# A hybrid encoder layer on one core: residual rows and norm weights loaded with the output projection, values' stores held one round, two weight places added within the value group

## The chip, the cores and the metric

The kernel runs on one core of a Trainium2 chip. The metric is the time of one execution on the device, in microseconds, as the median of several runs. The engines are named as in the profile: PE is TensorE (matmuls and transposes), DVE is VectorE, ACT is ScalarE, POOL is GpSimd, SP is SyncE, which here only issues DMAs. POOL and ACT issue some DMAs too.

## What is computed

One encoder layer, for a prompt of 1024 tokens (A) and a sample of 512 tokens (B) with the same weights, in float32. The reference, cut to its frame:

```python
def encoder_layer(x, pre_w, w_in, conv_w, conv_b, i_bias, f_bias, head_norm_w, w_pm, w_pa, w_out, post_w, rel_table):
    h = rms_norm(x, pre_w)
    cols = jnp.einsum('bsd,dc->bsc', h, w_in)
    m_qk, m_v, m_o, m_z, m_i, m_f, a_qkv, a_z, gate = jnp.split(cols, np.cumsum(IN_SPLITS)[:-1], axis=-1)
    y_m = mlstm_mixer(m_qk, m_v, m_o, m_i, m_f, ...) * jax.nn.silu(m_z)
    y_a = dilated_attention(a_qkv, rel_table) * jax.nn.silu(a_z)
    p_m = jnp.einsum('bsc,cd->bsd', y_m, w_pm)
    p_a = jnp.einsum('bsc,cd->bsd', y_a, w_pa)
    g = jax.nn.sigmoid(gate).reshape(b_, s_, N_BRANCHES, D_MODEL)
    merged = g[:, :, 0] * p_m + g[:, :, 1] * p_a
    out = jnp.einsum('bsd,de->bse', merged, w_out)
    return x + rms_norm(out, post_w)
```

The model is 1024 wide; the combined input projection gives queries, keys and values for a bidirectional mLSTM (4 heads of 256) and for attention in three dilation groups of 8 heads of 64, and the gates. "Values" below are the columns of `m_v` and of the attention's v. The residual rows are the `x` of the last line; the last norm's weights are `post_w`.

## The kernel before

Every large product is made of three matmuls with operands split in a high and a low part (`mm3`, L199 to L203): high times high, high times low, low times high. A weight is therefore loaded as raw float32 (`load_w`), copied to its high part on ACT (L261) and subtracted to its low part on DVE (L265); both are in `split_w`, which keeps the two instructions in `self.splits`. Raw weights have two buffers, `wraw`; split weights rotate through a list of places, `wsplit`, three by default: the front one is taken and put back at the end. `retired` lists places that are dropped when they come to the front.

The program has two halves. First A's input projection runs dense. Then follows a part in which the attention and the mLSTM of one batch form a main thread, and dense work of the other is the *fill*: A's mLSTM, A's attention, B's mLSTM, B's attention, and the end, with `STEPS` = 316, 260, 192, 290 and 86 fill steps planned for each. A fill step is three matmuls of a weight unit. `Fill.stage` spreads a stage's steps over its shares, and `fill(share)` runs the steps that have come due. The fill's order is: B's input projection in units of 8 steps, 40 of them ahead of B's values; the values (192 steps); the rest of B's projection, to step 768 (`SHORT`); then for each block of 512 tokens the two branch projections (`branches`) and the output projection (`final`).

`Fill.load` splits further weights ahead of their use: never more than `ahead` (2; 4 in the last two stages) beyond those taken, and never more than there are places. `base` counts the weights that are no longer needed.

The values (`value_units`) come in six groups of 430 columns. A group has four weights, each for two of the eight contraction blocks, and four token tiles; `slot` walks through tiles and weights so that the next tile begins two slots after the one before it. The four weights of a group stay until its last tile has used them, and so the group needs more places than three. Two more come from the arena tiles `X0` and `X1`, free between A's mLSTM and B's. When a token tile has its eight blocks, `put` in `value_units` copies it from PSUM to `sw` (L779 and L786 on ACT, L780 on DVE) and stores it to `vs` (mLSTM values, high and low part) or `av` (attention values). `sw` is a rotation of four buffers, shared with the other units. A PSUM bank (two for `dense`) is free only after these copies.

Stores in these stages are not issued at once. `Net.put` appends them to `pending` with the round at which they become due, `clock + lag`; `lag` is 2 or 3, in the attention 3. `tick`, at the start of every round of the main thread, issues the queued loads of that round and then the stores that have come due (L217). A store is issued earlier if its buffer's turn in the rotation comes again.

The main thread of the attention (`attend`, `att_round`) has 96 rounds for A and 48 for B. A round computes the logits of one tile (`lg`, L1308), the softmax of the tile before (L1320, L1322 on DVE, L1324 on ACT), transposes the probabilities of the one before that (`pt`, L1331; copied to `pts`, L1334 or L1336), runs its share of fill and makes the output of the oldest (`o`, L1343; L1345). A unit of two heads has 8 rounds in A; the loads for the next unit are queued in a unit's second round and spread over the rest.

The order of work is fixed by hand for PE and SP: they follow the program's order (`manual_schedule`). For ACT, DVE and POOL a planner chooses at compile time, from what is ready in its own simulation. `tc.issue_after(ins)` adds, for each instruction that its block traces on the engine of `ins`, an ordering edge behind `ins`; it orders the issue alone, without a wait, and leaves other engines' instructions as they are.

`side` is the queue on which weights, merge gates, branch rows and residual rows are loaded: SP, but POOL during A's attention and from B's attention on. In the last two stages the pool `out` (`osb`) holds the tiles of the branches and of the output projection, among them `postw`, the norm's weights broadcast to 128 partitions and scaled by ACT (L1907, L1908).

In `final`, a token tile's output has two halves of 512 columns, u = 0 and 1; `close` takes each from PSUM (L1630, L1632, L1637 use `pw`, which is `postw`), and after the second half adds the residual rows `xo` (L1640), which were loaded by L1666 when that half's first contraction blocks were done.

## Time and profile before

| what | value |
|---|---|
| runs | 2278.32, 2275.62, 2276.38 us; median 2276.38 us |
| the profiled execution's own time | 2276.12 us |
| its span, first to last instruction | 2274.3 us |
| granted TensorE clock, mean | 0.998 |
| DMA moved | 418.80 MB, 184 GB/s over the span |
| A's attention, about | 1300 to 1650 us of the span |
| B's values within it | 1351.2 (first L779) to 1580.8 us (last L786) |
| B's attention begins, about | 1845 us |

A row of the timeline gives start, duration, engine and line, what is written from what, and in brackets how long the engine was idle before it and which event ended that. A row of waits gives total, count and longest, in us. A "q" behind an engine's name is its instruction queue. A row for a tile or line gives the least, median and greatest duration in ns, and the first and last start. In the windows view a stretch's length is followed by the busy time of PE, of PE's weight loads, of DVE, ACT and POOL, then the granted clock, the DMA engines' busy share and GB/s.

### The profile page before, as it was taken

How to read it: one execution, taken by the hardware profiler on the slowest of the kernel's cores; microseconds unless marked ns; L12 is line 12 of the kernel's file. 1: busy time of each engine (PE TensorE's matmuls, PEld its weight loads, DVE VectorE, ACT ScalarE, POOL GpSimd, SP SyncE). 2: the span in 40 equal slices, each digit the busy share in tenths (PEclk: the TensorE clock that was granted, in tenths of full speed). 3: DMA queues.
4: the chain of work that ended last, by engine and by line, in shares of the span. 5: the costliest groups of instructions: out<-in, count | busy, mean ns of one | idle time of the engine just before them, and what ended most of it. 6: DMA issues, size and time to landing. Idle time of an engine off the chain costs nothing.

```text
span 2274.3 us, 35427 instructions
## 1 busy us (share of the span) xinstructions
PE 2249.4 (99%) x12226; PEld 1966.9 (86%) x12226; DVE 1505.8 (66%) x2865; ACT 1131.9 (50%) x2368; POOL 723.4 (32%) x1004
## 2 busy tenths in 40 slices
PE   9999999999999999999999999999999999999998
PEld 8999888888888888888888889899888888888887
DVE  6765577677776556467887845444689844655774
ACT  6432244344444334366777655566666644555332
POOL 2000333343333223237666611011065522221230
PEclk9999999999999999999999999999999999999999
DMA  3652555543333223394674589987678787776672
GB/s 122 170 130 78 172 207 194 192 169 119 111 110 108 82 81 136 112 329 130 220 230 143 164 231 252 218 236 226 199 259 282 225 274 232 228 244 195 222 252 84
DMA packets 223213, 418.80 MB, mean 184 GB/s; under 512 B 24857, under 2 KB 129497, under 8 KB 223034
## 3 DMA queue, kind: packets, MB, share of 16 engines
q1 hardware_dynamic: 195064, 316.21, 44.1%
q0 software_dynamic: 24368, 87.74, 12.2%
q10 hardware_dynamic: 3602, 12.59, 1.4%
q8 instruction: 97, 1.59, 0.3%
q14 instruction: 82, 0.67, 0.1%
HBM read 296.45 MB, written 128.39 MB: 187 GB/s over the span
## 4 chain that ended last, share of the span: by engine, by line
PE 87%; DMA 6%; DVE 2%; issue 2%; POOL 2%; ACT 1%; SPq 0%; DVEq 0%; POOLq 0%; ACTq 0%
PE d L203 13%; PE d L201 13%; PE d L202 13%; PE dense L201 10%; PE dense L203 10%; PE dense L202 10%; PE o L1343 4%; PE pt L1331 2%; PE lg L1308 2%; PE num L203 1%; PE num L201 1%; PE num L202 1%; DMA wraw<-w_in 1%; PE kv L201 1%; PE kv L202 1%
## 5 line engine op out<-in xcount | busy, mean ns | idle before, releaser
L201 PE MATMUL dense<-H,wh 128*128 128x512 f32 x664 | 270.4, 407 | 2.7 <-ACT sw L850 2.7
L203 PE MATMUL dense<-H,wl 128*128 128x512 f32 x664 | 260.8, 393 | 0.0
L202 PE MATMUL dense<-H,wh 128*128 128x512 f32 x664 | 260.3, 392 | 0.0
L202 PE MATMUL d<-Hl,phla 128*128 128x512 f32 x608 | 236.5, 389 | 0.0
L203 PE MATMUL d<-Hh,phla 128*128 128x512 f32 x608 | 236.5, 389 | 0.0
L201 PE MATMUL d<-Hh,phla 128*128 128x512 f32 x608 | 236.5, 389 | 0.0
L265 DVE TENSOR_TENSOR wl<-wraw,wh 128x1024 fp32r<-128x1024 f32 (+1 forms) x121 | 148.6, 1228 | 105.8 <-ACT wh L261 103.1
L203 PE MATMUL d<-Hh,phlb 128*128 128x512 f32 x456 | 177.4, 389 | 0.0
L201 PE MATMUL d<-Hh,phlb 128*128 128x512 f32 x456 | 177.4, 389 | 0.0
L202 PE MATMUL d<-Hl,phlb 128*128 128x512 f32 x456 | 177.4, 389 | 0.0
L648 POOL TENSOR_TENSOR psum_w<-pw_raw 128x512 f32<-128x512 f32 x38 | 59.1, 1556 | 368.7 <-DMA pw_raw<-w_in 343.5
L261 ACT ACTIVATE wh<-wraw 128x1024 fp32r<-128x1024 f32 (+1 forms) x124 | 128.5, 1036 | 94.2 <-PE dense L202 25.8
L1324 ACT ACTIVATE ls<-ls,nm 128x256 f32<-128x256 f32 (+1 forms) x288 | 130.1, 453 | 84.9 <-DVE nm L1322 64.0
L1320 DVE CUSTOM_DVE_ANT_0 ls<-lg,bias 128x256 f32<-128x256 f32 (+1 forms) x288 | 93.5, 361 | 118.7 <-PE lg L1308 48.9
L203 PEld LDWEIGHTS dense<-H,wl 128*128 128x128 f32 x664 | 124.7, 188 | 28.2
L201 PE MATMUL d<-vhi,Hh 128*128 128x322 f32 x448 | 140.9, 314 | 0.3
L203 PE MATMUL d<-vhi,Hl 128*128 128x322 f32 x448 | 140.2, 313 | 0.4 <-DVE Hl L370 0.2
L201 PEld LDWEIGHTS dense<-H,wh 128*128 128x128 f32 x664 | 125.0, 188 | 17.3 <-ACT sw L850 2.9
L202 PE MATMUL d<-vlo,Hh 128*128 128x322 f32 x448 | 139.6, 311 | 0.0
L202 PEld LDWEIGHTS dense<-H,wh 128*128 128x128 f32 x664 | 125.4, 189 | 14.3
L201 PEld LDWEIGHTS d<-Hh,phla 128*128 128x128 f32 x608 | 114.1, 188 | 23.7
L203 PEld LDWEIGHTS d<-Hh,phla 128*128 128x128 f32 x608 | 114.1, 188 | 23.7
(564 smaller groups left out, 6169.7 us busy)
## 6 DMA issues: line engine op xcount, KB each, us to landing
pw_raw<-w_in SPq DMA_DIRECT2D x76, 512.0 KB
wraw<-w_in SPq DMA_DIRECT2D x64, 512.0 KB
aqk_a<-pwk SPq DMA_DIRECT2D x48, 512.0 KB
aqk_b<-sw SPq DMA_DIRECT2D x48, 256.0 KB
wraw<-w_pm POOLq DMA_DIRECT2D x24, 512.0 KB, 6.3
wraw<-w_out POOLq DMA_DIRECT2D x24, 512.0 KB, 4.4
wraw<-w_v POOLq DMA_DIRECT2D x23, 430.0 KB, 5.9
erep<-erow SPq DMA_DIRECT2D x16, 512.0 KB
```

Of the source, the lines that this page charges most:

```text
L201: nc.tensor.matmul(out, lh, rh, start=start, stop=False)
L202: nc.tensor.matmul(out, lh, rl, start=False, stop=False)
L203: nc.tensor.matmul(out, ll, rh, start=False, stop=stop)
L261: high = nc.scalar.activation(hi[:, :n], raw[:, :n], AF.Copy)
L265: low = (self.lows or nc.vector).tensor_sub(lo[:, :n], raw[:, :n], hi[:, :n].bitcast(F32))
L648: self.nc.gpsimd.tensor_add(s[:, 0], ws[1][:, 0], ws[1][:, 1])
L1308: nc.tensor.matmul(lg[:, hh, c:c + w], q[hh][:, qs], z[:, k0:k0 + w], start=z is k[hh], stop=z is not k[hh])
L1320: nc.vector.tensor_tensor_reduce(out=ls[:, hh], in0=ts["lg"][hh], in1=bt[:, hh], scale=1.0, scalar=NEG, op0=OP.add, op1=OP.max, accum_out= ...
L1324: nc.scalar.activation(ls[:, hh], ls[:, hh], AF.Exp, bias=nm[:, hh:hh + 1], accum_out=ot[:, 128 + hh:129 + hh])
L1331: nc.tensor.transpose(pp[:, hh * nk + x], ts["ls"][:, hh, x * P:(x + 1) * P], self.ident)
L1343: nc.tensor.matmul(po[:, hh * 64:hh * 64 + 64], pt[:, hh * nk + x], v[:, kt[x], c0 + hh * 64:c0 + hh * 64 + 64], start=x == 0, stop=x == n ...
```

## The change

There are four edits. `put` takes a `lag` of its own, and the three stores of `value_units` pass 1. The places in `X0` and `X1` are taken at slot 1 of the value unit, and are inserted into `wsplit` behind its free places, instead of being appended after A's mLSTM; `retired` is set from a local list. The residual rows' loads stand in `issue_after(self.splits[1].ins)`. The norm's weights are no longer loaded on SP ahead of B's attention, but in the first `final`, on `side`, in the same kind of block; their tile is allocated there, and ACT scales it there.

```diff
-    def put(self, key, out, src, of, queue=None):
+    def put(self, key, out, src, of, queue=None, lag=None):
         if self.defer:
-            self.pending.append((self.clock + self.lag, key, (out, src), self.owner.get(id(of))))
+            self.pending.append((self.clock + (lag or self.lag), key, (out, src), self.owner.get(id(of))))
...
-                    self.put(("vs", T.S), T.vs[i, ts, a0 - 16:a1 - 16], z.bitcast(F32), parts[i])
+                    self.put(("vs", T.S), T.vs[i, ts, a0 - 16:a1 - 16], z.bitcast(F32), parts[i], lag=1)
...
-                self.put(("av", T.S), T.av[ts, a0 - 16 - D:hi - 16 - D], z[:, :hi - a0], z)
+                self.put(("av", T.S), T.av[ts, a0 - 16 - D:hi - 16 - D], z[:, :hi - a0], z, lag=1)
...
             for slot in range(8 * groups + 2):
+                if slot == 1:
+                    x = [self.take(x) for x in ("X0", "X1")]
+                    free = len(self.wsplit) - (len(fill.ready) - fill.base)
+                    self.wsplit[free:free] = [[z[:, 1024 * i:1024 * (i + 1)] for i in range(2)] for z in x]
+                    extra = [z[0] for z in self.wsplit[free:free + 2]]
...
-            self.retired = self.extra
+            self.retired = extra
...
+            if self.postw is None:
+                self.postw = sb.tile([P, D], F32, name="postw")
+                with self.tc.issue_after(self.splits[1].ins):
+                    self.side.dma_start(self.postw, a["postw"][0:1].to_broadcast([P, D]))
+                nc.scalar.mul(self.postw, self.postw, math.sqrt(D))
             pw = self.postw
...
                             for hf, x in enumerate(xo[t][1]):
-                                self.side.dma_start(x, T.x[b * BLK + t * P:b * BLK + (t + 1) * P, hf * BLK:(hf + 1) * BLK])
+                                with self.tc.issue_after(self.splits[1].ins):
+                                    self.side.dma_start(x, T.x[b * BLK + t * P:b * BLK + (t + 1) * P, hf * BLK:(hf + 1) * BLK])
...
                 N.side = nc.gpsimd
-                extra = [N.take(x) for x in ("X0", "X1")]
-                extra = [[x[:, 1024 * i:1024 * (i + 1)] for i in range(2)] for x in extra]
-                N.extra = [x[0] for x in extra]
-                N.wsplit += extra
...
-            N.postw = N.osb.tile([P, D], F32, name="postw")
-            nc.sync.dma_start(N.postw, a["postw"][0:1].to_broadcast([P, D]))
-            nc.scalar.mul(N.postw, N.postw, math.sqrt(D))
+            N.postw = None
```

More of the change, by code (lines that the diff above doesn't have):

```diff
@@ L189, in __init__ @@
         self.scans = []
-        self.extra, self.retired = [], []
+        self.retired = []
         self.narrow, self.acc = {}, [None, None]
```

## The prediction

> **What bounds the kernel now.** I read the page first: engine shares, then the chain that ended last.
>
> ```profile
> span 2274.3 us, 35427 instructions
> PE 2249.4 (99%) x12226; PEld 1966.9 (86%) x12226; DVE 1505.8 (66%) x2865; ACT 1131.9 (50%) x2368; POOL 723.4 (32%) x1004
> PE 87%; DMA 6%; DVE 2%; issue 2%; POOL 2%; ACT 1%; SPq 0%; DVEq 0%; POOLq 0%; ACTq 0%
> ```
>
> TensorE is busy all but 24.9 us (2274.3 − 2249.4), and the change leaves every matmul in place. So it can gain only from idle PE time in the stages it touches, and from a lowered clock. The view of waits names the PE stalls there.
>
> ```profile
> PE dense L201 <- ACT sw L850: 2.7, 1, 2.7
> PE dense L201 <- ACT sw L786: 2.5, 2, 1.7
> ```
>
> L786 belongs to the sample batch's values, which run as fill during the attention of A; L850 runs where the attention of B begins. Stretches around both, in the windows view (columns: stretch, its length, then each engine's busy time and count, PE clock, DMA share, GB/s):
>
> ```profile
> 1444.00:1448.00 4.00, 3.15 (x21) 2.74 (x21) 1.20 (x6) 1.38 (x5) 0.00 (x0) 1.00 0.68 150
> 1468.00:1472.00 4.00, 1.69 (x7) 1.32 (x8) 3.20 (x12) 2.06 (x7) 0.55 (x1) 0.91 1.03 225
> 1472.00:1476.00 4.00, 4.00 (x19) 3.92 (x19) 1.61 (x7) 3.90 (x15) 0.00 (x0) 0.50 1.08 230
> 1476.00:1480.00 4.00, 4.00 (x24) 3.84 (x23) 0.88 (x5) 3.93 (x10) 0.00 (x0) 0.74 0.99 222
> 1840.00:1844.00 4.00, 4.00 (x19) 3.31 (x18) 0.00 (x0) 0.00 (x0) 0.21 (x1) 1.00 1.04 412
> 1844.00:1848.00 4.00, 1.43 (x9) 1.07 (x7) 0.40 (x1) 1.49 (x2) 0.00 (x0) 1.00 1.03 416
> 1848.00:1852.00 4.00, 3.89 (x17) 3.23 (x18) 2.73 (x5) 2.66 (x4) 1.18 (x3) 1.00 1.07 279
> ```
>
> The reader is to see three holes: 0.85 us near 1447; a longer one at 1467 to 1471, after which the granted clock is 0.50 and then 0.74; one of 2.7 us at 1845 to 1848, after which it stays 1.00. The lowered clock costs (1 − 0.50) × 4 + (1 − 0.74) × 4 = 3.0 us.
>
> **The values' stores.** The first hole, from the timelines of VectorE, SyncE's queue and ScalarE, and the chain of waits, whose DMA rows run from issue to landing:
>
> ```profile
> 1432.31 0.35 DVE L780 TENSOR_TENSOR sw<-dense,sw 128x180 fp32r<-128x180 f32 x1 [0.29 <-ACT sw L779]
> ...
> 1438.09 1.10 SPq L217 DMA_DIRECT2D vs_b<-sw  x2
> ...
> 1438.87 7.67 DMA vs_b<-sw
> ...
> 1446.62 0.38 ACT L786 ACTIVATE sw<-dense 128x250 f32<-128x250 f32 x1 [2.84 <-DMA vs_b<-sw]
> ...
> 1447.05 0.47 PE L201 MATMUL dense<-X,H 128*128 128x430 f32 x1 [0.85 <-ACT sw L786]
> ```
>
> The data of a token tile are ready at 1432.66 (1432.31 + 0.35), but the stores, held three rounds, are issued at 1438.09 and 1438.87, and the second takes 7.67 us to land. Only then may the next tile reuse its place of the four in `sw`, and PE waits for the PSUM bank behind that copy. With lag 1 SyncE reaches the stores before the data: they go at 1432.66 plus two issues, 1433.8 at the latest. Landing after another 7.67 us, at 1441.5, they are ahead of the 1443.78 (1446.62 − 2.84) at which ScalarE stood ready. **The 0.85 us go.** What is late next is the second hole.
>
> ```profile
> 1454.72 1.05 SPq L217 DMA_DIRECT2D vs_b<-sw  x2
> ...
> 1459.77 0.55 POOL L253 DMA_DIRECT2D wraw<-w_v  x1 [1.32 <-DVE wl L265]
> ...
> 1463.11 0.35 DVE L780 TENSOR_TENSOR sw<-dense,sw 128x180 fp32r<-128x180 f32 x1 [2.70 <-DMA vs_b<-sw]
> ...
> 1467.82 0.92 ACT L261 ACTIVATE wh<-wraw 128x860 fp32r<-128x860 f32 x1 [5.86 <-DMA wraw<-w_v]
> ...
> 1468.77 1.05 DVE L265 TENSOR_TENSOR wl<-wraw,wh 128x860 fp32r<-128x860 f32 x1 [5.32 <-ACT wh L261]
> ...
> 1469.22 0.46 PE L201 MATMUL dense<-wh,H 128*128 128x430 f32 x1 [1.68 <-ACT sw L786]
> ...
> 1470.42 0.69 DVE L1336 COPY pts<-pt 128x512 f32<-128x512 f32 x1
> ...
> 1471.17 1.92 PE L1343 MATMUL o<-K,pts 128*128 128x64 f32 x8 [1.09 <-DVE pts L1336]
> ```
>
> Here ScalarE stands at L261 for a weight that took 8.05 us to land (1459.77 to 1467.82). Behind L261 on ScalarE is the L786 for which PE waits 1.68 us; behind L265 on VectorE is the copy for which PE waits 1.09. With the clock the hole is worth 1.68 + 1.09 + 3.0 = 5.8 us. Bounds for the change: nothing, since the first wait, if L786 now passes ahead of L261, only hands over to the second, whose end hangs on the same landing; and 5.8, if the weight lands 3 us sooner. In between: the stores of 1454.72 move to about 1452.9, out of the crowd in which the weight lands. If it lands 1.1 us sooner (an estimate: the issue of those two stores, 1.05 us, no longer ahead of it), PE idles 2.77 − 1.1 = 1.7 us, nearer to the hole of 2.7 us at 1848 that kept its clock than to this one; so I take 1.1 + 3.0 = 4.1 us. This is the least certain term.
>
> The Trainium skill, "TensorE: Matmul & The Clock Gate", section "What's actually happening", has the clock fall to half after one idle window of about 3.4 us, free-running. The trace agrees in kind: 0.50 after the scattered 2.77 us, 1.00 after 2.68 in one piece. By that rule shortening the hole at all can save the 3.0 us, or save none, by where the window falls.
>
> What lag 1 adds: SyncE, one queue in order, waits at each store until ScalarE and VectorE have written. Behind it stand attention loads, bias rows and outputs of the next ticks.
>
> ```profile
> L217 SPq DMA_DIRECT2D vs_b<-sw x24: 319/379/580, 1354.3 to 1472.6; - x24
> ...
> L217 SPq DMA_DIRECT2D av_b<-sw x16: 319/376/530, 1440.0 to 1582.4; - x16
> ...
> 1437.55 0.45 SPq L242 DMA_DIRECT2D V1b<-aqk_a  x1
> ...
> 1455.10 0.36 PE L1308 MATMUL lg<-V1a,Q 128*128 128x256 f32 x1
> ...
> 1458.67 0.36 PE L1308 MATMUL lg<-V1a,Q 128*128 128x256 f32 x1
> ```
>
> The 40 stores keep their number and bytes; their issues move within one queue. The last keys of a unit go out at 1437.55 and are first used at 1455.10, 17.5 us later; less 7.67 for landing, 9.9 us of cover. A round is 3.57 us (1455.10 to 1458.67), so two rounds of hold take at most 7.1 of them. **Cost taken: 0**; without that cover, a rival below.
>
> **The two places.** `X0`, `X1` join `wsplit` at slot 1 of the value unit instead of after A's mLSTM. From the code: that stage is staged for 316 steps in 73 shares and hands out 70.33 (4 of lead, 2 in the first `prepare`, 64 − 8/3 in the rounds, 3 after them), so 304 steps, exactly 38 units. Two more units and slot 0 take three weights, rotating the old three places once round; the appended pairs then stand first, which is where the new insertion (`free` = 3 − 3 = 0) puts them. No load before slot 1 may run further ahead than three (`ahead` is 2). Same places, same order: 0 us, both bounds 0, unless the planner places another engine's work otherwise, which I leave to the range.
>
> **Residual rows.** `issue_after` orders only instructions of its argument's engine, and without a wait. The argument is the VectorE subtraction of L265; the loads are issued by POOL. No edge arises: 0 us, and the early loads stay.
>
> ```profile
> L1666 POOL DMA_DIRECT2D xo<-x_prompt x12: 536/538/586, 1834.8 to 2146.3; - x12
> ...
> L1632 DVE TENSOR_TENSOR sw<-dense,postw x12: 682/687/692, 1979.6 to 2248.9; 128x512 f32<-128x512 f32 x12
> ```
>
> POOL's order is the planner's, not the program's: rows go out at 1834.8, although the projection they belong to closes its first tile at 1979.6.
>
> **The norm's weights.** Their load moves from SyncE to POOL under the same edge that does not arise, so I expect it where the planner puts ready POOL loads, at 1835.
>
> ```profile
> 1834.81 2.12 POOL L1666 DMA_DIRECT2D xo<-x_prompt  x4
> ...
> 1835.95 1.46 SPq L253 DMA_DIRECT2D wraw<-w_in  x2
> 1837.58 0.36 SPq L1907 DMA_DIRECT2D postw<-postw  x1
> ...
> 1846.51 1.06 ACT L261 ACTIVATE wh<-wraw 128x1024 fp32r<-128x1024 f32 x1 [10.05 <-DMA wraw<-w_in]
> 1847.48 0.58 ACT L850 ACTIVATE sw<-dense 128x512 f32<-128x512 f32 x1
> ...
> 1850.27 1.06 ACT L1908 ACTIVATE postw<-postw 128x1024 f32<-128x1024 f32 x1 [0.80 <-DMA postw<-postw]
> ```
>
> These rows are the third hole: the weight issued at 1835.95 lands at 1846.51 amid the crowd, and L850 stands behind its split. The load is 128 × 1024 × 4 B = 524 KB, at 412 GB/s (row 1840 to 1844) 1.27 us. Today it is issued behind that weight; in front of it, it can delay it by 1.27 us at most, and where the queues share by turns by next to nothing: 0 to +1.3. The other way, SyncE loses one issue (0.36 us) and POOL gains one about as long as a residual load (0.54); ScalarE's multiplication (1.06) finds 10 idle us ahead of 1846.51. I take +0.2, nearer the low end, since POOL's loads of 1834.81 are in flight with the weight already.
>
> Sum, against the profiled execution's 2276.12 us (span 2274.3 and 1.8 around it; the median of the three runs is 2276.38, 0.3 higher): 2276.1 − 0.85 − 4.1 + 0 + 0 + 0.2 = **2271.4 us**.
>
> **Rivals.** *Only the first hole closes*: the weight lands no sooner, the clock still falls. For it: 1469 hangs on that landing in both its waits. 2276.1 − 0.85 + 0.2 = 2275.5.
>
> *SyncE's hold makes the attention wait* (slower). At each store the queue stands until the copies are done; it decides once landing takes longer than 17.5 − 7.1 = 10.4 us, as the weight of 1835.95 shows it can (10.6). Against it: 7.67 here. The values cover 192 of 260 fill steps, so 12 × 192/260 = 8.9 unit starts, a third of them behind a store that holds two rounds: 3 starts, about 1 us each, and one fall of the clock, 3.0: with no gain at 1469, 2275.5 + 6 = 2281.5.
>
> *The norm's weights go in front and the clock falls at 1848*: 2.7 + 1.3 = 4.0 us of hole, more than the 2.77 that was followed by 0.50, so 3.0 more: 2275.5 − 0.2 + 1.3 + 3.0 = 2279.6.
>
> *The change does what its words say*: residual rows (4 × 256 KB) and norm weights leave the crowd; 1.57 MB at 412 GB/s is 3.8 us, more than the hole's 2.7. 2271.4 − 0.2 − 2.7 = 2268.5. Against it: no edge, above. A different memory place for the tiles could still do it.
>
> **How the numbers follow.** Forecast 0.42, within 2269 to 2273.5 (the weight's 1.1 us doubled or halved); only the first hole 0.15; SyncE's hold, or another stall of its kind, 0.23; clock at 1848 0.10; as the words say 0.10. A run of this kernel tells 0.2% (4.6 us) from no change: below 2271.8 is faster, above 2280.9 slower. Of the forecast 0.30 lies below and 0.12 within; with the last case faster is 0.40. Within: 0.12 + 0.15 + half of 0.10 = 0.32. Slower: 0.23 + 0.05 = 0.28. The range runs from 2267 (below the last case) to 2283 (above the hold's 2281.5).
>
> **What would show it.** `vs_b` stores issued within 1.2 us of L780's end; no wait of L786 on `vs_b`; near 1469 a clock of 1.00 and less than 2 us idle. SyncE's waits on `sw` should grow and no `lg` wait for keys. `xo` still issued near 1835, by POOL, and `postw` beside it. I am wrong if PE idles at unit starts, if the clock is 0.50 anywhere new, or if the rows move to 1930 and later.

## The result, and the profile after

The changed kernel takes 2280.75 us (median of 17 runs, 2278.14 to 2287.97) against 2275.2 us for the kernel before in the same series (17 runs, 2269.97 to 2280.55): a ratio of 1.0026, 95% interval [1.0018, 1.0034]. It is slower by 0.26%, where 2271.4 us and a gain were forecast. A second series gave 2281.93 us (12 runs) and 1.0029 [1.0016, 1.0042]. The profiled execution took 2280.61 us, so it stands for the median well. Below, "the changed kernel" means this one. In it some lines of the code have moved: 850 is now 855, 1143 is 1148, 1324 is 1329, 1331 is 1336, 1526 is 1531, 1666 is 1677; 1632 is now the load of the norm's weights and 1642 the product that was 1632.

Its page, the first lines:

```profile
span 2278.8 us, 35411 instructions
PE 2251.1 (99%) x12226; PEld 1965.5 (86%) x12226; DVE 1504.5 (66%) x2865; ACT 1130.3 (50%) x2368; POOL 724.1 (32%) x1005
```

PE's idle time is 2278.8 − 2251.1 = 27.7 us, 2.8 more than before; the other 1.7 of the 4.5 us count as busy, with the same 12226 matmuls. The view of waits says where the idle time is now:

```profile
PE dense L201 <- ACT sw L855: 4.5, 1, 4.5
PE dense L201 <- ACT sw L786: 0.6, 1, 0.6
```

The wait for L786 in A's attention fell from 2.5 to 0.6 us; the one wait for L855, where B's attention begins, rose from 2.7 to 4.5. The windows view of the same stretches:

```profile
1444.00:1448.00 4.00, 4.00 (x30) 3.94 (x30) 0.95 (x5) 2.31 (x9) 0.00 (x0) 1.00 0.83 198
1468.00:1472.00 4.00, 2.90 (x23) 2.68 (x22) 3.13 (x16) 2.60 (x10) 0.55 (x1) 1.00 0.85 242
1472.00:1476.00 4.00, 4.00 (x29) 3.92 (x28) 0.71 (x3) 3.88 (x12) 0.00 (x0) 1.00 1.05 228
1844.00:1848.00 4.00, 0.29 (x3) 0.08 (x1) 0.00 (x0) 0.81 (x1) 0.00 (x0) 0.90 1.02 409
1848.00:1852.00 4.00, 3.22 (x8) 2.55 (x9) 3.10 (x6) 3.22 (x5) 2.04 (x3) 0.50 1.02 250
1852.00:1856.00 4.00, 4.00 (x17) 3.28 (x16) 0.24 (x3) 1.09 (x4) 0.93 (x3) 0.75 1.04 259
```

The hole at 1447 is gone (4.00 us of PE in 4.00). The one at 1469 is shorter and no lowered clock follows it (1.00). But behind the hole at 1848 the clock is now 0.50 and then 0.75, which costs (1 − 0.50) × 4 + (1 − 0.75) × 4 = 3.0 us: the fall of the clock has moved from 1472 to 1848.

The timeline of the changed kernel in the values shows that the stores do what was forecast. Behind it stand a row of its chain of waits, from issue to landing, and a row of the timeline of before:

```profile
1432.67 0.80 SPq L217 DMA_DIRECT2D vs_b<-sw  x2
1432.68 0.35 DVE L780 TENSOR_TENSOR sw<-dense,sw 128x180 fp32r<-128x180 f32 x1 [0.29 <-ACT sw L779]
...
1457.15 0.55 POOL L253 DMA_DIRECT2D wraw<-w_v  x1 [4.71 <-DVE X L265]
1459.67 0.55 POOL L253 DMA_DIRECT2D wraw<-w_v  x1 [1.98 <-DVE wl L265]
...
1465.94 0.92 ACT L261 ACTIVATE wh<-wraw 128x860 fp32r<-128x860 f32 x1 [4.34 <-DMA wraw<-w_v]
```

```profile
1457.15 8.77 DMA wraw<-w_v
```

```profile
1457.89 0.55 POOL L253 DMA_DIRECT2D wraw<-w_v  x1 [4.71 <-DVE X L265]
```

The stores leave with L780 instead of 5.4 us behind it. The weight that makes the hole at 1469 is the one issued at 1457.15: raw weights have two buffers and are split in the order of their loads, and the chain has this load landing at 1465.92, where L261 starts. The load of 1459.67 is the next one. In the same way L261 at 1467.82 in the kernel before waited for the load of 1457.89, not for that of 1459.77, which the prediction read. So the weight lands 8.79 us after its issue (1465.94 − 1457.15) instead of 9.93 (1467.82 − 1457.89), that is 1.14 sooner, and it is also issued 0.74 earlier. And the timeline around B's attention:

```profile
1833.14 0.53 POOL L1632 DMA_DIRECT2D postw<-postw  x1
1833.67 2.13 POOL L1677 DMA_DIRECT2D xo<-x_prompt  x4
1833.71 0.58 ACT L855 ACTIVATE sw<-dense 128x512 f32<-128x512 f32 x1
1834.25 2.20 SPq L217 DMA_DIRECT2D ym_b<-ym  x2
1836.50 3.74 SPq L253 DMA_DIRECT2D wraw<-w_in  x2
...
1847.19 1.06 ACT L261 ACTIVATE wh<-wraw 128x1024 fp32r<-128x1024 f32 x1 [11.87 <-DMA wraw<-w_in]
1848.15 0.58 ACT L855 ACTIVATE sw<-dense 128x512 f32<-128x512 f32 x1
```

Both sets of loads are at 1833 to 1836, the rows 1.1 us earlier than before: the ordering edges of the change hold nothing back. Two rows of the timeline of before that the prediction does not show:

```profile
1834.39 1.50 SPq L217 DMA_DIRECT2D ym_b<-ym  x2
1834.84 0.58 ACT L850 ACTIVATE sw<-dense 128x512 f32<-128x512 f32 x1
```

Compare, in times of the span. The weight is issued 0.55 us later (1836.50 against 1835.95), since SyncE spent 2.20 us and not 1.50 on the two stores ahead of it. It lands 0.68 later (1847.19 against 1846.51). PE, which gained upstream, is there earlier by about the 1.13 us by which the last copy before the hole is earlier (1833.71 against 1834.84). Together 1.8 us: the 2.7 us became 4.5. The weight's flight, from issue to landing, hardly changed (10.69 us against 10.56). What grew is the time from that copy to the weight's issue, 2.79 us against 1.11. Only 1.8 us of that is waiting; crossing from a hole that the clock outlived to one that it did not costs 3.0 more.

### The profile page after: what moved, and what is told of

Read it like the earlier page. It is cut to its first block, busy times and chain, and to the rows that moved or that the text cites. A ratio compares the mean times of both kernels' runs of the same rounds, so it can differ in the third digit from the quotient of the medians.

```text
span 2278.8 us, 35411 instructions
## 1 busy us (share of the span) xinstructions
PE 2251.1 (99%) x12226; PEld 1965.5 (86%) x12226; DVE 1504.5 (66%) x2865; ACT 1130.3 (50%) x2368; POOL 724.1 (32%) x1005
## 4 chain that ended last, share of the span: by engine, by line
PE 81%; DMA 7%; issue 5%; DVE 3%; POOL 2%; ACT 2%; SPq 0%; POOLq 0%; DVEq 0%; ACTq 0%
PE d L203 13%; PE d L202 13%; PE d L201 13%; PE dense L201 9%; PE dense L202 9%; PE dense L203 9%; PE o L1348 2%; DMA wraw<-w_v 2%; PE pt L1336 1%; PE lg L1313 1%; PE num L203 1%; PE num L201 1%; PE num L202 1%; DMA wraw<-w_in 1%; DMA vs_a<-vz 1%
## 5 line engine op out<-in xcount | busy, mean ns | idle before, releaser
L265 DVE TENSOR_TENSOR wl<-wraw,wh 128x1024 fp32r<-128x1024 f32 (+1 forms) x121 | 149.7, 1237 | 92.3 <-ACT wh L261 90.3
L261 ACT ACTIVATE wh<-wraw 128x1024 fp32r<-128x1024 f32 (+1 forms) x124 | 128.4, 1035 | 86.4 <-PE dense L202 25.9
L201 PEld LDWEIGHTS d<-Hh,phla 128*128 128x128 f32 x608 | 114.1, 188 | 23.7
L202 PEld LDWEIGHTS d<-Hl,phla 128*128 128x128 f32 x608 | 114.1, 188 | 23.7
```

The lines of the kernel that those rows point to most:

```text
L201: nc.tensor.matmul(out, lh, rh, start=start, stop=False)
L202: nc.tensor.matmul(out, lh, rl, start=False, stop=False)
L261: high = nc.scalar.activation(hi[:, :n], raw[:, :n], AF.Copy)
L265: low = (self.lows or nc.vector).tensor_sub(lo[:, :n], raw[:, :n], hi[:, :n].bitcast(F32))
```

## The experiments

Each table line below is one profiled execution. The numbers are worked out from the traces, not a view of the profile: for each pair of neighbouring matmuls, the distance from start to start less the median of that distance for such pairs, summed in a stretch where it is over 0.1 us. It counts idle time and a lowered clock together. "Stores 1" means held one round, "early" or "held" is where rows and norm's weights are.

```
                                      span  1421  1447  1469  1507  1693  1848  1881  all
before                              2274.3  0     1.11  5.87  0     0.93  2.94  0     24.5
the change                          2278.8  0.58  0     2.07  0.41  2.43  7.20  0     29.2
 again                              2279.2  1.50  0     3.37  0     2.45  6.41  0     28.8
 a third time                       2284.7  1.13  0     5.41  0     2.43  6.71  0     34.1
stores 1 alone                      2271.1  1.06  0     2.05  1.01  0.84  0     0     20.7
 again                              2269.9  1.32  0     0.58  0     2.43  1.82  0     20.1
 third                              2273.3  1.43  0     2.62  0.63  2.42  0.24  0     23.0
 fourth                             2274.3  1.36  0     2.04  0.77  0.85  5.03  0     24.5
norm's load alone                   2283.0  0     0.34  4.34  0     0.85  7.04  0     32.2
norm's load, tile at its old place  2272.3  0     0.36  4.38  0.22  0.88  1.89  0     23.3
tiles moved, no load moved          2275.0  0     0.57  5.64  0     0.89  2.47  0     25.2
stores 1 + norm's load, old place   2272.0  1.11  0     3.36  0.19  2.43  0     0     21.2
rows held alone                     2274.1  0     0     3.91  0     0.90  0     1.91  24.3
stores 1 + rows held                2274.5  1.43  0     2.08  0.42  2.42  0     0     24.4
the change, norm held               2272.8  1.06  0     2.67  0.22  2.44  0.90  0     21.8
the change, rows held               2271.5  0.93  0     1.97  0.37  0.85  1.38  0.65  20.9
the change, both held               2273.4  0.69  0     4.02  0     0.88  0     0.63  22.9
stores 2 alone                      2272.2  0.36  0     2.17  0     0.84  2.53  0     23.0
both held, stores 2                 2272.6  0     0     1.78  0     2.44  0     0     22.5
 again                              2267.6  0.42  0     1.22  0.22  0.83  0     0     16.9
```

The change against before, first profiles: +4.3 at 1848, −3.8 at 1469, −1.1 at 1447, +1.0 at 1421 and 1507 together, +1.5 at 1693, and +2.8 in smaller holes elsewhere, which differ from execution to execution; 4.7 in all. Single executions of one kernel differ by 3 to 15 us within a series, and some of the profiles are far from their kernel's median: norm's load alone and the change a third time are the slowest of their twelve, "stores 1 + norm's load, old place" is the quickest. So the table tells where the holes are; how much an edit costs is taken from the timed series. The two places in `wsplit`, and the ordering edge on the residual rows as the change has it, were not run by themselves. But "stores 1 + norm's load, old place" has neither, and in its trace every engine runs the same instructions in the same order as in the change; so neither of the two moves an instruction.

**Stores alone.** The kernel before with the change's `lag=1` and nothing else.

```diff
-                    self.put(("vs", T.S), T.vs[i, ts, a0 - 16:a1 - 16], z.bitcast(F32), parts[i])
+                    self.put(("vs", T.S), T.vs[i, ts, a0 - 16:a1 - 16], z.bitcast(F32), parts[i], lag=1)
...
-                self.put(("av", T.S), T.av[ts, a0 - 16 - D:hi - 16 - D], z[:, :hi - a0], z)
+                self.put(("av", T.S), T.av[ts, a0 - 16 - D:hi - 16 - D], z[:, :hi - a0], z, lag=1)
```

> The kernel before with the values' stores held one round; nothing else is changed. Theory 1 (the loss sits where B's attention begins, and comes from the norm's load): the holes near 1447 and 1469 us shrink as in the changed kernel, the hole at 1848 stays near 2.7 us at a clock of 1.00, and the time is 4 to 5 us under the kernel before (ratio about 0.998). Rival A (SyncE's hold costs the loss): at or above the kernel before, 1.000 to 1.003. Rival B (what is gained upstream is lost again at 1848, because PE only arrives earlier at a landing that does not move): hole at 1848 of 4 us or more, a clock of 0.50 behind it, and a time within 1 us of the kernel before.

2278.24 us (12 runs) against 2274.46 for before (35 runs), ratio 1.0005 [0.9992, 1.0019]: no gain. A second series, of eight, has 2277.58 us and 1.0012 [1.0001, 1.0023]. The time is that of rival A; the profile shows the smaller holes of theory 1. The executions fall in two groups, five at 2271.19 to 2273.0 and seven at 2278.18 to 2281.39; the profile is one of the lower.

**Norm's load alone.** The kernel before with the change's load of `postw` in `final` and its tile allocated there.

```diff
+            if self.postw is None:
+                self.postw = sb.tile([P, D], F32, name="postw")
+                with self.tc.issue_after(self.splits[1].ins):
+                    self.side.dma_start(self.postw, a["postw"][0:1].to_broadcast([P, D]))
+                nc.scalar.mul(self.postw, self.postw, math.sqrt(D))
...
-            N.postw = N.osb.tile([P, D], F32, name="postw")
-            nc.sync.dma_start(N.postw, a["postw"][0:1].to_broadcast([P, D]))
-            nc.scalar.mul(N.postw, N.postw, math.sqrt(D))
+            N.postw = None
```

> The kernel before with the norm's weights allocated and loaded in the first output projection, on POOL, as in the changed kernel; the stores as before. Theory 1: the load goes out near 1834 us ahead of the residual rows, the hole at 1848 is 4 us or more and the clock falls to 0.50 behind it, holes at 1447 and 1469 as before; 5 us or more slower, ratio 1.002 to 1.004. Rival A: no change, 1.000. Rival B: the hole grows by no more than 1.3 us and the clock stays, ratio 1.000 to 1.001.

2278.07 us (12 runs, 2271.68 to 2284.75), ratio 1.0016 [1.0001, 1.0031]: slower by 3.6 us in the median, by the term that I took at +0.2, though less than theory 1 had forecast. Its profile has 7.04 us at 1848, as the change, but it is of the slowest of the 12 executions (2284.75).

**The place of its tile.** In the change `postw` is allocated last in its pool and the merge gates' tiles take its old place. The first kernel has the load of the change but the old place; the second has the load of before and the new places.

```diff
+            N.postw = N.osb.tile([P, D], F32, name="postw")
+            N.postw_due = True
```

> As the norm's weights alone, loaded on POOL in the first output projection, but their tile keeps its old place in memory, so that the merge gates' tiles keep theirs; every engine's order is that of the norm alone. If the load itself makes the loss: as the norm alone, 1.002 to 1.004. If the moved tiles make it (a merge gate's load that no longer waits for memory goes out 8 us earlier, among the stores of B's mLSTM): the first gate load stands near 1833 us again, the hole at 1848 is near 3 us, and the ratio 1.000 to 1.001.

2274.84 us, ratio 1.0002 [0.9991, 1.0014], with 1.89 us at 1848.

```diff
+            for name, bufs, shape in (("gab", 3, [P, BLK]), ("mg", 2, [P, BLK]), ("ss", 2, [P, 4, 8])):
+                for _ in range(bufs):
+                    N.osb.tile(shape, F32, name=name, bufs=bufs)
             N.postw = N.osb.tile([P, D], F32, name="postw")
```

> The kernel before with the order of all engines, but with the tiles of the merge gates, the merged rows and the sums allocated ahead of the norm's weights, as in the changed kernel; the load stays on SyncE. If the load itself makes the loss: 1.000, hole at 1848 of 2.7 us. If the moved tiles make it: one merge gate is loaded near 1825 us, VectorE's wait for the store of ym_a grows from 2.0 us, the hole at 1848 reaches 4 us with a lowered clock, ratio 1.002 to 1.003.

2275.97 us, ratio 1.0004 [0.9992, 1.0016]. So neither half is slower by itself that can be told, and together they are; the three intervals overlap, so that the place matters is possible and not shown. A second pair says the same, the change with the tile at its old place:

> The stores held one round and the norm's weights loaded on POOL as in the change, but their tile keeps the place in memory that it had before, so the merge gates' tiles keep theirs too. Theory 1 (the load needs the moved tiles to hurt, since only then does one gate load pass ahead and the weights go out with it): the load costs no more than with before's stores (2274.84 against 2274.46), so the time is that of the stores alone, medians between 2271.5 and 2278.5 in two groups. Theory 2 (stores and load together make the hole, place or no place): 2280 to 2281, as the change, with 6 us or more at 1848.

2277.27 us, ratio 1.0013 [1.0002, 1.0024], between the stores alone and the change; its profile, of the quickest of its 12 executions, shows nothing at 1848. There is a reading in it that the bytes alone do not give:

```profile
1833.94 2.15 SPq L253 DMA_DIRECT2D wraw<-w_in  x2
1834.12 0.53 POOL L1627 DMA_DIRECT2D postw<-postw  x1
1834.65 2.12 POOL L1670 DMA_DIRECT2D xo<-x_prompt  x4
...
1841.67 1.06 ACT L261 ACTIVATE wh<-wraw 128x1024 fp32r<-128x1024 f32 x1 [5.88 <-DMA wraw<-w_in]
```

The same loads as in the change go out beside the weight, but here the weight is issued 0.18 us ahead of the first of them, and it lands after 7.73 us. In three profiles of the change it is issued 2.4 to 3.4 us behind the first, and lands after 10.6 to 11.9.

**Rows and weights truly held.** The change with one name added, so that the edge is on an instruction of POOL, which issues these loads:

```diff
-        self.side.dma_start(raw[:, :kt * cols], src)
+        self.lastload = self.side.dma_start(raw[:, :kt * cols], src)
...
-                with self.tc.issue_after(self.splits[1].ins):
+                with self.tc.issue_after(self.lastload.ins):
```

> The change with its order made true: the residual rows and the norm's weights are ordered behind the load of the last projection weight, an instruction of the engine that issues them, so none of them goes out at 1833 to 1836. Everything else is as in the changed kernel, SyncE's order too. Theory 1 (what keeps the changed kernel slow is the crowd of loads in front of and beside the weight of 1836, whose late landing makes the hole of 7.2 us at 1848): hole at 1848 under 1 us, clock 1.00, time about 2280.75 - 6.5 = 2274. Theory 2 (the tiles' new places make it slow, whatever the order): the hole stays over 4 us, time 2278 to 2281. Theory 3 (rows that come late make their own waits in the projection): a new wait of VectorE on xo near 1979 or 2248, and 2276 or more.

2274.37 us (12 runs, 2272.33 to 2278.56), ratio 0.9999 [0.9989, 1.001]: six us below the change, and its interval lies below the change's. Two views of it, the rows of the residual rows' line and the timeline at B's attention:

```profile
L1677 POOL DMA_DIRECT2D xo<-x_prompt x12: 536/536/581, 1999.2 to 2148.9; - x12
```

```profile
1836.28 3.55 SPq L253 DMA_DIRECT2D wraw<-w_in  x2
...
1843.58 1.06 ACT L261 ACTIVATE wh<-wraw 128x1024 fp32r<-128x1024 f32 x1 [6.92 <-DMA wraw<-w_in]
```

The rows go out at 1999.2 at the earliest, and the weight lands 7.30 us after its issue (1843.58 − 1836.28) instead of 10.69, so PE does not wait at 1848 at all. This is theory 1. The edge does more than hold the loads: from 1847 on, behind this landing, the planner also places a number of instructions of ACT, DVE and POOL otherwise than in the change. So the closed hole is the held loads' work, and how much of the six us is due to the new order is not told apart.

> The kernel before with one edit: the residual rows are ordered behind the load of the last projection weight, so 4 x 256 KB leave the time from 1835 to 1846. Theory 1 (they delay the weight of 1836): the hole of 2.9 us at 1848 shrinks below 1 us and the time falls by 2 us, 2272.5 against 2274.5. Theory 2 (their share of the queues is not what delays it): hole 2 to 3 us, time within 1 us of before.

The same edge for the rows alone, in the kernel before: 2276.44 us, ratio 1.0006 [0.9994, 1.0019]. The hole at 1848 closes (0), but 1.91 us open at 1881 and the median does not fall: theory 1 is right on the hole and wrong on the time.

**Two kernels profiled again.** Stores alone three times more, and the change again.

> The stores alone once more, for a second profile. The executions fall in two groups, near 2272.3 and near 2278.6. Theory 1 (PE reaches B's first copies earlier than the weight of 1836 allows, and the clock gate falls or does not): a profile of the upper group shows 3 to 5 us idle at 1845 to 1850 and a clock of 0.50 behind it, where the first profile, of the lower group, showed none; one of the lower group shows none again. Theory 2 (the hole at 1469 decides): the upper group has its 0.50 at 1470 and nothing at 1848.

> The stores alone a third time, one profiled execution. Of 20 executions so far 6 lie at 2271.2 to 2273.0 and 14 at 2276.4 to 2281.4, with the same mean clock of 0.999 in most of both, so the upper ones must idle some 5 us longer and not run slower. Theory 1: an upper execution shows these 5 us at 1843 to 1850, where the copy behind the weight of 1836 is waited for (0 and 1.8 us in the two profiles, both of lower executions). Theory 2: they lie elsewhere, at 1469 or in the first 1300 us that no edit touches. A lower execution again (2271 to 2273) tells nothing new.

> As the third: theory 1 has an upper execution idle about 5 us at 1843 to 1850, theory 2 elsewhere; a lower one has under 2 us at 1848.

> The changed kernel once more, for a second profile: theory 1 (the hole at 1848 is its mark) expects 5 us or more of it with the clock, at 2279 to 2285; theory 2 (the first profile was an accident) expects under 3 us there and the loss elsewhere.

The profiled executions of the stores alone took 2271.63, 2275.1 and 2276.13 us; the seven timed beside the first of them took 2276.42 to 2279.15. The second profile of the change took 2280.99, with 6.41 us at 1848: theory 1. Of the four profiles of the stores alone the last and slowest has a hole at 1848 as theory 1 wants it (5.03), with a lower clock; the windows view of it and then of the first, which has none:

```profile
1840.00:1844.00 4.00, 2.38 (x13) 1.86 (x11) 0.00 (x0) 0.00 (x0) 0.00 (x0) 1.00 1.03 420
1844.00:1848.00 4.00, 2.39 (x8) 1.90 (x9) 2.69 (x3) 3.94 (x5) 0.54 (x1) 0.88 1.05 340
1848.00:1852.00 4.00, 4.00 (x16) 3.28 (x15) 1.20 (x5) 1.18 (x5) 1.75 (x4) 0.70 1.06 270
```

```profile
1840.00:1844.00 4.00, 4.00 (x21) 3.38 (x20) 1.23 (x1) 2.07 (x3) 0.33 (x1) 1.00 1.03 416
1844.00:1848.00 4.00, 4.00 (x19) 3.30 (x18) 1.62 (x3) 2.08 (x3) 0.73 (x2) 1.00 1.06 361
```

So the same program meets that hole or not, with the weight's flight 10.9 us in the one and 8.0 in the other. What goes with it can be read from the four traces: how long behind the first residual row (POOL's L1666) the weight is issued on SyncE (worked out from the timelines, in us).

| profile | weight's issue behind the first row | its flight | hole at 1848, from the table |
|---|---|---|---|
| first | −0.20 | 7.95 | 0 |
| third | −0.09 | 9.10 | 0.24 |
| again | 0.66 | 9.9 at most | 1.82 |
| fourth | 1.40 | 10.87 | 5.03 |

The bytes are the same in all four. The rows go out within 0.05 us of the last copy ahead of the hole (L850), so a late issue behind them also means that PE is early. Four profiles are no experiment, and no kernel changes this order alone; whether the order is the cause stays open. And none of the four is one of the upper executions near 2278, so what makes those stays open.

**Why the stores gain nothing.** The table shows a new hole at 1421 in every profile with stores held one round (0.58 to 1.50) and in none with three; at 1507 in most of the first and once, with 0.22, in the others. The timeline of the stores alone, first profile, then that of before:

```profile
1411.71 0.55 POOL L253 DMA_DIRECT2D wraw<-w_v  x1 [10.26 <-DVE X L265]
1412.52 1.27 SPq L217 DMA_DIRECT2D vs_b<-sw  x2
...
1420.21 0.92 ACT L261 ACTIVATE wh<-wraw 128x860 fp32r<-128x860 f32 x1 [5.77 <-DMA wraw<-w_v]
...
1421.68 0.93 PE L1331 MATMUL pt<-ident,ls 128*128 128x128 f32 x4 [0.68 <-ACT ls L1324]
```

```profile
1411.10 0.55 POOL L253 DMA_DIRECT2D wraw<-w_v  x1 [11.59 <-DVE X L265]
...
1417.97 0.92 ACT L261 ACTIVATE wh<-wraw 128x860 fp32r<-128x860 f32 x1 [4.14 <-DMA wraw<-w_v]
1418.64 1.01 SPq L217 DMA_DIRECT2D vs_b<-sw  x2
```

Before, the stores left 0.7 us after the weight had landed; held one round they leave 0.8 us after it was issued, and it lands after 8.50 us (1420.21 − 1411.71) instead of 6.87. ScalarE stands at L261 for it, behind it in ScalarE's order is the exponential of the attention (L1324), and PE waits for that. It is the same kind of crowd as at 1454, in another group.

> The stores held one round and the residual rows ordered behind the load of the last projection weight, the norm's weights as before. Theory 1 (both holes are landings of one weight in a crowd): 1469 under 2.1 us, 1848 under 1 us, 0.6 to 1.9 us new at 1881 as in the two kernels with held rows, and a median near 2271 to 2273. Theory 2 (each hole closed opens another by as much): 2274 to 2276, as before.

Stores one round and rows held, norm's weights as before: 2276.91 us, ratio 1.0004 [0.9994, 1.0015]. Theory 2: with 1848 closed it is still not faster.

**Which load, and how long a hold.** The change with only the norm's weights held, with only the rows held, as it is, and with both held and the stores at two rounds (`lag=2`), all four in one series where before took 2274.56 us.

> The change, with its norm's weights truly ordered behind the last projection weight; the residual rows stay early, beside the weight of 1836. Theory 1 (the norm's 524 KB in front of the weight are what the change adds there): the hole at 1848 falls from 7.2 to what the stores alone show, 0 to 5 us, and the time to 2276 to 2278. Theory 2 (rows and an early PE suffice): it stays over 5 us, 2279 to 2281.

> The change, with its residual rows truly held and the norm's weights left early. Theory 1 (the norm's weights alone make 4 us or more of the hole): still over 3 us at 1848 and 2278 to 2281. Theory 2 (it is the bytes in all, and four rows of 262 KB, 1.05 MB, are twice the norm's 0.52 MB): under 2 us there, and 2274 to 2276.

> The changed kernel on the same chip as the three others: 2280 to 2282 by both theories, with 6 to 7 us at 1848.

> The kernel with rows and norm's weights truly held (2274.37 before), its values' stores held two rounds instead of one. Theory 1 (stores of one round fly with the next weight and give back 0.4 to 1.5 us at 1421 and 1507): those two holes gone, 1469 no worse than 4 us, and 1 to 2 us faster, 2272.5 to 2273.5. Theory 2 (each hold has its own collisions): other holes of the same sum, 2274 to 2277.

| kernel | median of 12, us | ratio to before | bytes beside the weight at 1835 | its flight, us |
|---|---|---|---|---|
| the change | 2281.93 | 1.0029 [1.0016, 1.0042] | rows and norm, 1.57 MB | 10.6 |
| norm held | 2279.79 | 1.0015 [1.0001, 1.0029] | rows, 1.05 MB | 9.47 |
| rows held | 2276.45 | 1.0006 [0.9993, 1.0018] | norm, 0.52 MB | 8.70 |
| both held, stores two rounds | 2272.35 | 0.999 [0.9978, 1.0001] | neither | 5.85 |

The flights are from the SyncE and ScalarE rows of each timeline; here are the two in the middle, norm held first:

```profile
1835.20 2.96 SPq L253 DMA_DIRECT2D wraw<-w_in  x2
...
1844.67 1.06 ACT L261 ACTIVATE wh<-wraw 128x1024 fp32r<-128x1024 f32 x1 [8.01 <-DMA wraw<-w_in]
```

```profile
1833.19 1.36 SPq L253 DMA_DIRECT2D wraw<-w_in  x2
...
1841.89 1.06 ACT L261 ACTIVATE wh<-wraw 128x1024 fp32r<-128x1024 f32 x1 [8.48 <-DMA wraw<-w_in]
```

In time, norm held is theory 2 (rows and an early PE suffice) and rows held is nearest to its theory 2 (the bytes in all); both held with stores at two rounds is theory 1. Time and flight fall with the bytes beside the weight in these four, and by the medians the four rows matter more than the norm's weights. But each flight is of one execution: the profile of the change is of its slowest (2286.43 us), that of norm held 4.9 us below its median. Flights range from 8.0 to 10.9 us at the same bytes in the stores alone, and one of 7.73 us had all 1.57 MB beside it (above); so bytes are part of it and do not set it alone. In the last kernel the stores changed too, and its executions lie within 3.0 us of each other (2271.32 to 2274.35), where the change spreads over 10.

That kernel again, and its hold of two rounds without the rest:

> Rows and norm's weights truly held, stores held two rounds, a second time. Theory 1 (it removes the holes at 1421, 1447, 1507 and 1848 and shortens 1469): 2271.5 to 2273.5 with a spread of 3 us, 1.5 to 2.5 below before. Theory 2 (the first time was a lucky group): as before, 2274 to 2276.

> The kernel before with one edit: the values' stores held two rounds. Theory 1 (the stores of two rounds are the gain at 1447 and 1469, and the loads at 1835 still make their hole): 1469 under 3 us and no holes at 1421 and 1507, but 2 to 5 us at 1848, so 2273 to 2277 with a wide spread. Theory 2 (the stores are all of it): 2272 to 2273, as with the rest.

2270.18 us (11 runs, 2268.79 to 2272.22) against 2273.72, ratio 0.9983 [0.9974, 0.9992]: it is faster than the kernel before, and so than the change: theory 1 again. Two rounds alone: 2271.49 us, 0.9989 [0.998, 0.9998], nearer to theory 2; so the longer hold is most of it, though the rows and weights are not told apart from nothing (the intervals overlap). The timeline of the best version at the group of 1411, and its waits:

```profile
1411.84 0.55 POOL L253 DMA_DIRECT2D wraw<-w_v  x1 [10.25 <-DVE X L265]
...
1417.55 1.52 SPq L217 DMA_DIRECT2D vs_b<-sw  x2
1419.70 0.92 ACT L261 ACTIVATE wh<-wraw 128x860 fp32r<-128x860 f32 x1 [5.12 <-DMA wraw<-w_v]
```

```profile
PE dense L201 <- ACT sw L786: 0.8, 1, 0.8
PE pt L1336 <- ACT ls L1329: 0.2, 1, 0.2
```

The stores of this group leave 5.7 us after the weight, which takes 7.86 us to land: longer than before (6.87), shorter than with one round (8.50). PE's waits for L786 and for the exponential come to 1.0 us; for L855 there is none. Two rounds still empty `sw` in time at 1447 (0 in the table).

At 1469 the gain has another source. The timeline of two rounds alone, whose lines are numbered as in the kernel before:

```profile
1465.23 0.69 DVE L1336 COPY pts<-pt 128x512 f32<-128x512 f32 x1
1469.44 0.92 ACT L261 ACTIVATE wh<-wraw 128x860 fp32r<-128x860 f32 x1 [5.16 <-DMA wraw<-w_v]
1470.39 1.05 DVE L265 TENSOR_TENSOR wl<-wraw,wh 128x860 fp32r<-128x860 f32 x1 [4.48 <-ACT wh L261]
1471.37 1.00 PE L1343 MATMUL o<-K,pts 128*128 128x64 f32 x8
```

The planner now places the copy L1336 ahead of L265 and not behind it, so PE no longer waits 1.09 us for it (no wait at 1471.37), and no lowered clock follows. The weight itself lands no sooner in two of the three profiles with two rounds: its flight is 9.9 and 10.0 us there and 9.2 in the third, against 9.93 before.

## Why the prediction was wrong

**The first hole, −0.85**: right. It is gone in every profile with stores held one or two rounds, and the stores leave with L780, as forecast.

**The second hole, −4.1**: right in mechanism, and in size where the clock held, though with a misread row: the weight is the load of 1457.89 with a flight of 9.93 us, not that of 1459.77 with 8.05. Its flight fell by 1.14 us (1.1 was the estimate), and in the first profile of the change PE idles 0.56 + 1.10 = 1.66 us there (1.7 was forecast); that an estimate made for another load fits so closely is in part luck. The stores alone show 0.58 to 2.62 us there against 5.87, at a clock of 1.00. But one of three profiles of the change still has 5.41 and another 3.37, each with a lowered clock. The Trainium skill, "TensorE: Matmul & The Clock Gate", section "What's actually happening", has the clock fall after one idle window of about 3.4 us, free-running. These profiles agree with it in so far as one kind of hole is followed by a fall in some executions and not in others; that less than 3.4 us of scattered idle time can be enough, these profiles show and that section does not say.

**SyncE's hold, taken at 0**: this is the first step that failed, and the larger one. I asked which attention loads stand behind the stores in SyncE's queue, and found 9.9 us of cover for the keys; that held, and no `lg` in A's attention waits for keys. I did not ask which weights of the other groups are in flight when the stores leave earlier, though that was my argument for the hole at 1469. At 1421 the weight takes 1.6 us longer to land; with 1507 this gives back 2.1 us in three of the four profiles of the stores alone and 1.3 in the other. The stores alone were forecast at 2276.1 − 4.95 = 2271.2. Their four profiled executions reach 2271.63 to 2276.13, yet the first series has a median of 2278.24, with an interval from a gain of 0.08% to a loss of 0.19%, and the second a loss of 0.12%: some 1 to 3 us above before where 4.95 below were forecast. The give-back of about 2 us shows in the traces, and in the three profiles with two rounds it is 0 to 0.64; what makes the rest, in the upper executions, stays open. A wait at 1693 that is 1.5 us longer, in about half the profiles with earlier stores, is not explained either.

**The two places and the residual rows, 0 each**: right as to order, which neither of them changes (above); neither was timed alone. The rows left at 1833.7 in the change, since the edge is on a VectorE instruction; with the edge on one of POOL they left at 1999.2.

**The norm's weights, +0.2 with bounds 0 to +1.3**: this is the second step that failed. Alone it costs 3.6 us in the median (interval 0.01% to 0.31%). The bounds priced the landing, and in the change the weight does land only 0.68 us later. They took the hole to grow by as much and the clock to stay at 1.00. But the hole is the time between PE's arrival and the landing: PE came about 1.13 us earlier, and the hole passed from 2.7 us, which kept the clock, to 4.5, which did not. The bounds also left out that the tile's new place may do something, which two pairs of runs suggest.

**The rival** *the norm's weights go in front and the clock falls at 1848* is nearest to what happened: forecast a hole of 4.0 us, a clock cost of 3.0 and 2279.6; measured 4.5, 3.0 and 2280.75. That its time fits is in part luck. Its sum has no gain at 1469, where the first profile of the change gains 3.8, and nothing of the 1.0 at 1421 and 1507, the 1.5 at 1693 and the 2.8 in smaller holes; and with the norm's weights held and the rows early the change still takes 2279.79. It got 0.10 because it was taken as apart from the gain upstream. It is not: what PE gains there brings it earlier to a weight whose issue hangs on SyncE's stores, and about 1.13 of the 1.8 us by which the hole grew are this gain, spent as idle time; the fall of the clock comes on top. Of the signs that I had named, the stores at L780's end and a clock of 1.00 with under 2 us idle at 1469 came true, and so did one that would prove me wrong: a new place with 0.50.

**Rows and weights in the words' sense**, forecast at 2268.5: with the edge made true, 2274.37, 6 us below the change and level with before. The hole at 1848 closes as forecast, but up to 1.9 us open at 1881 in some of the profiles with held rows, and the stores' give-back remains. The Trainium skill, "DMA: Bandwidth & Descriptors", section "Queues, rings and completion order", says that each DMA engine takes packets in turn from the queues that have work. By that alone a load on POOL's queue would slow a weight on SyncE's whichever was issued first, and the order that I weighed, in front or behind, would matter less than the bytes. The flights of 10.6, 9.47, 8.70 and 5.85 us agree with that; the 7.73 us of a weight issued just ahead of the same 1.57 MB do not, nor do the 7.95 to 10.87 us of the stores alone at the same bytes.

## What to carry to other kernels

A store or load that is moved is to be priced at both ends of its move: by the wait that it leaves, and by the transfers in flight where it arrives, in every group of the loop and not only in the one with the hole. Here a hold of two rounds gained where one round did not, in part through an order that the planner found; so look also at what else an edit moves. When a hole stands near the length from which the clock falls (here 2.7 us in one piece kept it and 3.2 did not), an upstream gain is no gain until that hole is closed, since an engine that arrives earlier only waits longer. And an ordering edge acts on one engine here: look in the trace at which engine issues what is to be held, and at whether its issue time has moved, before anything is put down to the edge.

## What was not expected of the hardware

Holes in one piece of 2.2 to 2.7 us kept the clock at 1.00, in the profiles of before, of the moved tiles and of two rounds alone; 3.2 us in the fourth profile of the stores alone was followed by 0.88 and 0.70, and 4.3 to 4.7 us in three profiles of the change by rows of 0.50 to 0.75. Length alone does not decide it: at 1469 the 2.77 us before, in two pieces, were followed by 0.50, while 2.19 us in two pieces (1.10 and 1.09, the third profile of the stores alone) kept 1.00 and 1.75 (0.67 and 1.08, stores 1 with the norm's load at its old place) were followed by rows of 0.74 and 0.84. The weight of 1835, 524 KB, took 7.3 us to land with neither rows nor norm's weights beside it and the same stores and order on SyncE, against 10.6 to 11.9 in three profiles of the change: with 1.57 MB on another engine's queue it took 3.3 us or more longer, near the 3.8 that these bytes take at the 412 GB/s of that stretch (an estimate). But in the one profile where it was issued 0.18 us ahead of these loads it took 7.73.
